# The second output projection of a two-layer encoder as seven block products

## The chip, the cores and the metric

The kernel runs on one core of one Trainium2 chip. The metric is the device time of one execution in microseconds, a median of runs. Engines are named as in the profile: PE (TensorE matmul) with PEld (its weight loads), DVE (VectorE), ACT (ScalarE), POOL (GpSimd), SP (SyncE, which here only issues DMAs).

## What is computed

A trunk of two layers over a sequence of 1024 rows and a width of 1024. Each layer normalizes its input, modulates it with a vector made from c, runs a token mixer, multiplies by a SiLU gate, projects with a 1024x1024 matrix and adds the gated result to its input. Layer 0 mixes by differential attention, layer 1 by latent attention with 8 heads of 128. A last normalization closes the trunk:

```python
for i in range(DEPTH):
    shift, scale, gate = _modulation(c, ada_w[i], ada_b[i])
    h = _rmsnorm(x, norm_g[i]) * (1.0 + scale) + shift
    ...
        y = _mla(h, positions, w_in1, q_a_norm_g, w_q_b, kv_a_norm_g, w_kv_b, w_out1)   # ends in  o @ w_out
    x = x + gate * y
return _rmsnorm(x, final_norm_g)
```

The change concerns `o @ w_out1`, `x + gate * y` and the last normalization of layer 1. Here o (1024 x 1024) lies as eight heads of 128 features; the first 512 rows are called half 0, the others half 1.

## The kernel before

All matmuls with fp32 data are done as three products of split numbers: a value is rounded to fp32r (hi) and the rest (lo) kept, and `mm3` (L184 to L187) issues hi*hi, hi*lo and lo*hi into one accumulator bank. So every operand has to be split once: ACT casts it to hi, POOL or DVE subtracts to get lo. One step of `mm3` on a 128x128 piece of o and a 128x512 piece of the matrix is three matmuls of 128x512.

Layer 1's attention goes head by head. A head has two halves, a half four score tiles of 128 rows. A tile's work is: scores on PE (L1704), maximum on DVE (L400), exponential on ACT (L402), transposes on PE into one bank `tr` (L383), hi of the transposed tile on ACT (L385, `pth`), lo on DVE (L386, `ptl`), product with v on PE (`pv`). Between these PE does steps of the projections of the next head (`acc`, the weights split by L230 on ACT into `wh` and by L231 on POOL into `wl`). After each half the output o is scaled on POOL (L885), split (ACT L890, POOL L891), and stored to DRAM as hi and lo (`oS`). A generator is advanced once per score tile; it computes the gate vector of layer 1 in pieces (DVE L424) and ends about halfway through the heads.

During the last head `extra1` loads half 0 of o from `oS` and splits the first pieces of w_out1, and `Pre` does the first five contraction steps of two accumulators in PE's order beside that head's attention. `late1` and `tail1` finish the last half of the last head without DRAM: 1/z is made into a diagonal (`dg`), spread by a matmul with ones (`rb`, L904) and multiplied in.

Then `out_proj` runs over row halves (gi), column halves (f) and heads (h): four accumulators `oacc` of 128x512, and for each of the 4 x 8 pieces of the matrix a load (`wor`, L1088), a cast (`woh`, L1104) and a subtraction (`wol`, L1105). So each piece of w_out1 is loaded and split twice, once for each row half. When four accumulators are complete, DVE multiplies each with the gate (`oy`, L1152) and adds it to the residual `xfull` (L1153); `done1` squares and sums it on ACT (L1829), multiplies by the final gain on POOL (L1836), makes the reciprocal root in seven tiny DVE instructions (L178, L180, L181), scales one column half on DVE (L1843) and the other on ACT (L1850), and stores both. In the last quarter (`LAST`) the row tiles are done two together, then one, then the last tile in two pieces of 256 columns.

Every engine works through one queue in order; the order is made when the program is built, by a list scheduler that keeps to what `behind` (L192) and `in_turn` (L196) prescribe: some POOL instructions stay in program order, and casts on ACT go behind the attention's last marked cast or exponential. DMAs are issued by SP, which waits in order too.

Of the kernel before, what the change touches and what calls it, by code (L numbers as in the profile page):

```python
# [11 lines left out]
F32 = mybir.dt.float32  # L12
# [35 lines left out]
OT1_AT = 5  # L48
NORM_AT = 4
PRE0 = (0, 0, 0, 0, 0, 0, 1, 1, 1, 2, 1)  # L50
PRE1 = (0,0,0,0,0,0,1,1,1,1,1)
OW0 = (3, 4)
OP0 = (6, 4)
OW1 = (2, 4)
OP1 = (12, 4)
LAST = [(((0, 1, 2, 3), 0, HF),), (((0, 1), 0, HF), ((2,), 0, HF), ((3,), 0, 256), ((3,), 256, HF))]
# [30 lines left out]
def trunk(ctx: ExitStack, tc: tile.TileContext, A, out):  # L87
# [49 lines left out]
    oS = [dr.tile([NH, 2, 2, P, HF], F32, name=f"oS{l}") for l in range(2)]  # L137
# [46 lines left out]
    def mm3(psum, ah, al, bh, bl, first, last):  # L184
        PE.matmul(psum, ah, bh, start=first, stop=False)  # L185
        PE.matmul(psum, ah, bl, start=False, stop=False)  # L186
        mm3.last = PE.matmul(psum, al, bh, start=False, stop=last).ins  # L187
# [691 lines left out]
    def finish(o, y, l, h, half, dst, ap_, dgs):  # L879

        if dst is None:
# [6 lines left out]
            def split():  # L888
                with behind("S"):
                    S.copy(b.bitcast(F32R), o)  # L890
                in_turn(G.tensor_sub(o.bitcast(F32R), o, b))  # L891
                SP.dma_start(oS[l][h, half, 0], b)
                SP.dma_start(oS[l][h, half, 1], o)
# [6 lines left out]
        rb = bank("m", "rb")  # L900
# [4 lines left out]
        V.tensor_mul(o, o, rb)  # L905
        hi, lo = dst
# [219 lines left out]
    def out_proj(OT, ow, W0, pre, wpool, xpool, nlate, nx, xsrc, tile_done, group_done):  # L1126
# [4 lines left out]
        for gi in range(2):  # L1131
# [5 lines left out]
            for f in range(2):  # L1137
# [9 lines left out]
                last = gi == 1 and f == 1  # L1147

                def resid(i, a=0, b=HF, acc=None):
                    y = wpool.tile([P, HF], F32, name="oy", tag="oy", bufs=2)  # L1150
                    cs = slice(f * HF + a, f * HF + b)
                    V.tensor_mul(y[:, a:b], (acc or accs[i])[:, a:b], ow.gb[:, cs])  # L1152
                    add = V.tensor_add(fulls[i][:, cs], fulls[i][:, cs], y[:, a:b])  # L1153
                    tile_done(gi * 4 + i, fulls[i], cs.start, cs.stop, add)

                if last:
                    for tiles, a, b in LAST[ow.l]:
                        part = None
                        if a:
                            part = bank("acc", "oaccb")  # L1160
                        for h in range(NH):
                            for i in tiles:
                                mm_o(part or accs[i], OT, W, h, gi, i, slice(a, b))
                            if h % 2 or len(tiles) == 4:
                                side.tick()
# [770 lines left out]
```

## Time and profile before

| | us |
|---|---|
| median of 3 runs | 1436.38 (1433.73 to 1439.55) |
| the profiled execution | 1437.65 |
| its span in the profile | 1435.9 |
| PE busy | 1398.5 (97%) |
| DVE, ACT, POOL busy | 921.5, 727.2, 612.9 |

Numbers in the profile come from one execution; its time is 1.27 above the median of the runs, and 1.75 lie outside the span. In a group of instructions the first number is the time they were busy, the second the mean of one in ns. In a row of the timeline the first number is the start in us from the span's start, the second the duration. Matmuls overlap (the next begins before the one before has ended), so the price of a matmul on PE is the distance of two starts, not the duration. A number in square brackets is how long the engine stood idle just before, and for whom.

### The profile page before, as it was taken

Reading aid. Unit: us, or ns where it says so; the run is one execution under the profiler, and the core shown is the slowest. Engines: PE = TensorE matmul, PEld = TensorE weight load, DVE = VectorE, ACT = ScalarE, POOL = GpSimd, SP = SyncE. Lnnn points to the kernel's source line nnn. Section 1 sums busy time; section 2 is a strip of 40 time slices with the busy share of each in tenths; the row PEclk is TensorE's granted clock in tenths of the full one; section 3 lists DMA queues with packets and bytes.
Section 4 is the critical chain, followed back from the end, with each engine's and each line's share of the span. In section 5 each row is a group of like instructions: output and inputs, shape, how many; then the busy total and the mean of one; then the engine's idle time right before and its main releaser. Section 6 shows DMA issues by size and latency. Waiting matters only on the chain. (4 is left out here: it accounts for less than half of the span.)

```text
span 1435.9 us, 20702 instructions
## 1 busy us (share of the span) xinstructions
PE 1398.5 (97%) x7426; PEld 1165.9 (81%) x7426; DVE 921.5 (64%) x1377; ACT 727.2 (51%) x1287; POOL 612.9 (43%) x485
## 2 busy tenths in 40 slices
PE   9999999999999999998999999999999999999997
PEld 6777788888888887887787877887888888888886
DVE  8655777777777767677345985545666555555356
ACT  5523465656565655566343442345454454545342
POOL 5425264646464655454552234531141331412572
PEclk9999999999999999999999999999999999999999
DMA  9776533334342324237653146398343433336563
GB/s 343 244 242 204 185 89 107 82 110 118 103 111 85 104 77 112 58 96 263 230 175 125 37 133 205 123 299 242 112 135 106 135 105 82 97 102 205 185 237 135
DMA packets 135385, 213.18 MB, mean 148 GB/s; under 512 B 19057, under 2 KB 56049, under 8 KB 135282
## 3 DMA queue, kind: packets, MB, share of 16 engines
q1 hardware_dynamic: 135282, 211.86, 47.8%
q8 instruction: 58, 0.95, 0.3%
q14 instruction: 45, 0.37, 0.1%
HBM read 137.40 MB, written 50.80 MB: 131 GB/s over the span
## 5 line engine op out<-in xcount | busy, mean ns | idle before, releaser
L385 ACT CAST pth<-tr 128x512 fp32r<-128x512 f32 x256 | 150.3, 587 | 284.9 <-PE tr L383 283.1
L400 DVE TENSOR_REDUCE nm<-s 128x1 f32<-128x1024 f32 x192 | 233.9, 1218 | 69.9 <-PE s L847 58.4
L386 DVE TENSOR_TENSOR ptl<-tr,pth 128x512 fp32r<-128x512 f32 x256 | 176.0, 688 | 140.3 <-ACT pth L385 140.0
L231 POOL TENSOR_TENSOR wl<-wraw,wh 128x512 fp32r<-128x512 f32 (+2 forms) x79 | 105.1, 1333 | 205.1 <-ACT wh L230 170.1
L402 ACT ACTIVATE e<-s,nm 128x1024 f32<-128x1024 f32 x128 | 143.6, 1122 | 30.8 <-DVE nm L400 28.4
L383 PE MATMUL tr<-ident,e 128*128 128x128 f32 x1024 | 155.0, 274 | 2.5 <-DVE ptl L386 2.4
L383 PEld LDWEIGHTS tr<-ident,e 128*128 128x128 f32 x1024 | 121.1, 140 | 43.6 <-DVE ptl L386 19.4
L185 PE MATMUL acc<-h0h,wh 128*128 128x512 f32 x360 | 150.1, 417 | 1.0 <-DVE v_hl L363 1.0
L185 PE MATMUL pv<-pth,vt 128*128 128x256 f32 x512 | 147.6, 288 | 0.9 <-DMA vt<-vS 0.9
L186 PE MATMUL pv<-ptl,vt 128*128 128x256 f32 x512 | 145.7, 284 | 0.0
L187 PE MATMUL pv<-pth,vt 128*128 128x256 f32 x512 | 144.7, 283 | 0.0
L187 PE MATMUL acc<-h0h,wl 128*128 128x512 f32 x360 | 143.2, 398 | 0.6 <-POOL wl L231 0.6
L186 PE MATMUL acc<-h0l,wh 128*128 128x512 f32 x360 | 142.0, 394 | 0.0
L1105 POOL TENSOR_TENSOR wol<-wor,woh 128x512 fp32r<-128x512 f32 x64 | 85.5, 1358 | 84.9 <-ACT woh L1104 84.3
L185 PEld LDWEIGHTS pv<-pth,vt 128*128 128x128 f32 x512 | 97.4, 190 | 4.3 <-issue 1.1
L186 PEld LDWEIGHTS pv<-ptl,vt 128*128 128x128 f32 x512 | 97.6, 191 | 2.7
L187 PEld LDWEIGHTS pv<-pth,vt 128*128 128x128 f32 x512 | 97.6, 191 | 0.0
L847 PE MATMUL s<-ks,qa 128*128 128x512 f32 x256 | 82.6, 404 | 6.1 <-DVE e L855 4.4
L327 POOL TENSOR_TENSOR rp_r<-rp_raw,cosT 128x512 f32<-128x512 f32 x38 | 50.0, 1316 | 85.6 <-ACT rp_raw L324 38.6
L332 POOL TENSOR_TENSOR rp_sw<-rp_sw,sinT 128x512 f32<-128x512 f32 x42 | 55.2, 1314 | 73.2 <-DMA rp_sw<-rp_raw 73.1
L855 DVE SCALAR_TENSOR_TENSOR e<-s,z,e 128x1024 f32<-128x1024 f32 x64 | 82.1, 1283 | 2.1
L187 PEld LDWEIGHTS acc<-h0h,wl 128*128 128x128 f32 x360 | 67.6, 188 | 16.3 <-POOL wl L231 1.0
(599 smaller groups left out, 3370.9 us busy)
## 6 DMA issues: line engine op xcount, KB each, us to landing
ada<-in_ada_ss SPq DMA_DIRECT2D x32, 512.0 KB, 5.6
wraw<-in_w_s SPq DMA_DIRECT2D x64, 256.0 KB, 2.9
vS<-v_hl SPq DMA_DIRECT2D x32, 512.0 KB, 5.9
vt<-vS SPq DMA_DIRECT2D x32, 512.0 KB, 3.9
wor<-in_w_out SPq DMA_DIRECT2D x64, 256.0 KB, 3.6
rp_sw<-rp_raw SPq DMA_DIRECT2D x168, 64.0 KB, 2.0
bc_s<-bc_d SPq DMA_DIRECT2D x34, 256.0 KB, 4.2
oS<-bc_s SPq DMA_DIRECT2D x30, 256.0 KB, 2.4
```

Of the source, the lines that this page charges most:

```text
L185: PE.matmul(psum, ah, bh, start=first, stop=False)
L186: PE.matmul(psum, ah, bl, start=False, stop=False)
L187: mm3.last = PE.matmul(psum, al, bh, start=False, stop=last).ins
L231: sub = (V if pair_of else G).tensor_sub(l_[:, :n], raw[:, :n], f32v(h_[:, :n]))
L383: PE.transpose(tr[:, j, :], p[:, kt * P : (kt + 1) * P], ident)
L385: mk["S"] = S.copy(pth[kh][:, :, dst], tr).ins
L386: mk["V"] = V.tensor_sub(ptl[kh][:, :, dst], tr, f32v(pth[kh][:, :, dst])).ins
L400: mk["V"] = V.reduce_max(nm, s_ps, axis=AX.X, negate=True).ins
L402: mk["S"] = S.activation(e, s_ps, AF.Exp, bias=nm, scale=1.0, accum_out=zs).ins
L847: PE.matmul(s_ps[:, kc * HF : (kc + 1) * HF], src[:, c, ql], KS[h][kc][:, c, :], start=fst, stop=not fst)
L855: combined.append(V.scalar_tensor_tensor(out=e0, in0=e1, scalar=z1[:, 0:1], in1=e0, op0=ALU.mult, op1=ALU.add).ins)
L1105: in_turn(G.tensor_sub(lo, raw, f32v(hi)))
```

## The change

The product o @ w_out1 is cut into 2x2 blocks: o into row halves and into heads 0 to 3 and 4 to 7 (A11, A12 of half 0, A21, A22 of half 1), w_out1 into rows of the same head groups and two column halves (B11 to B22). It is computed with seven block products of 512x512x512 instead of eight, on sums of blocks (Winograd's form of Strassen's method). A block product is 4 contraction steps by 4 row tiles.

- The gate is multiplied into w_out1 beforehand. In heads 3 to 6 of layer 1, in the steps of the generator that were empty, w_out1 is loaded once, POOL multiplies it with the gate (L1632) and forms four sums (L1637 to L1643), and the seven blocks are stored to DRAM unsplit (`tS`, 28 pieces). The pieces of o are no longer split at the end of a half but stored once, unsplit (`oF`); for two of the four head pairs POOL forms the four sums (`pair_steps`, L1659 to L1662) in the same steps and they are stored (`sS`).
- In the last head the operands of block 0 and most of block 1 are loaded straight into the buffers that will hold lo, cast on ACT (L1859) and subtracted on POOL in place (L1860); the sums for the third head pair are made there too, those of the fourth pair by four DVE instructions after the last half is complete. `Pre7` does four contraction steps of two accumulators there.
- After the attention the blocks follow each other: block 0 and 2 in accumulators Y, 1 in Z, 3 and 4 in Z, 5 and 6 in Y. Y and Z are added to the residual (L1977) and not cleared between 0 and 2, 3 and 4, 2, 5 and 6, so that a product enters every output it belongs to. While a block runs, the operands of the next one are split (parts of o by DVE, of the matrix by POOL) and those of the one after it fetched.
- There is no gate multiplication any more behind the accumulators. Row tiles 0 to 3 are complete after block 4 and get one common reciprocal root on POOL; tiles 4 to 7 come at the end as before, with four contraction steps to a tile.

Three places show how the order of the work is moved. POOL, heads 5 and 6, where the last key weights are split; `wl` 128x256 is their lo part, the rows above it rope work (`rp_`) and the scaling of a half's output. Before:

```order
L327 TENSOR_TENSOR rp_r<-rp_raw,cosT 128x512
L332 TENSOR_TENSOR rp_sw<-rp_sw,sinT 128x512
L885 TENSOR_TENSOR o_12321<-o_12321,bc_s 128x512
L231 TENSOR_TENSOR wl<-wraw,wh 128x256
L891 TENSOR_TENSOR o_12321<-o_12321,bc_s 128x512
```

After, at the same place (`ob` and `ot` are pieces of w_out1, `gb` is the gate):

```order
L327 TENSOR_TENSOR rp_r<-rp_raw,cosT 128x512
L1632 TENSOR_TENSOR ob<-ob,gb 128x512 x4
L332 TENSOR_TENSOR rp_sw<-rp_sw,sinT 128x512
L1637 TENSOR_TENSOR ob<-ob 128x512
L1638 TENSOR_TENSOR ot_12394<-ob 128x512
L885 TENSOR_TENSOR o_12384<-o_12384,bc_s 128x512
L1642 TENSOR_TENSOR ob<-ot_12394,ob 128x512
L1643 TENSOR_TENSOR ob<-ob,ot_12394 128x512
L231 TENSOR_TENSOR wl<-wraw,wh 128x256
```

Eight instructions now stand between the rope product and the split of the weights; the subtraction behind it is gone.

ACT in the last head, two score tiles. Before:

```order
L402 ACTIVATE e,zz_12927<-s_13033,nm 128x1024
L1104 CAST woh<-wor 128x512
L385 CAST pth<-tr 128x4x128
L402 ACTIVATE e,zz_12927<-s_13071,nm 128x1024
L385 CAST pth<-tr 128x4x128
L890 CAST bc_s<-o_13020 128x512
L1104 CAST woh<-wor 128x512
```

After:

```order
L402 ACTIVATE e,zz_13009<-s_13130,nm 128x1024
L1859 CAST oah<-oal 128x512
L1859 CAST woh<-wol 128x512
L385 CAST pth<-tr 128x4x128
L402 ACTIVATE e,zz_13009<-s_13173,nm 128x1024
L385 CAST pth<-tr 128x4x128
L1859 CAST oah<-oal 128x512
L1859 CAST woh<-wol 128x512
```

Between the exponential and the next cast of the transposes stand two operand casts where there was one.

DVE at the end of the program, from the residual addition of tile 6. Before (`tw` sums of squares, `rq_y` and `rq_t` the reciprocal root):

```order
L1152 TENSOR_TENSOR oy<-oacc,gb 128x512
L1153 TENSOR_TENSOR xfull<-xfull,oy 128x512
L1838 SCALAR_TENSOR_TENSOR tw_13463<-tss,tw_13463 128x1
L178 TENSOR_SCALAR rq_y<-tw_13463 128x1
L1152 TENSOR_TENSOR oy<-oacc,gb 128x256
L180 TENSOR_SCALAR rq_t<-tw_13463,rq_y 128x1
L1153 TENSOR_TENSOR xfull<-xfull,oy 128x256
```

After, from the same addition:

```order
L1977 TENSOR_TENSOR x_6_13561<-x_6_13561,oy 128x512
L180 TENSOR_SCALAR rq_t<-tw_13569,rq_y 128x1
L1977 TENSOR_TENSOR x_7_13562<-x_7_13562,oy 128x256
L181 SCALAR_TENSOR_TENSOR rq_y<-rq_t,rq_y 128x1
L2007 SCALAR_TENSOR_TENSOR x_5_13560<-x_5_13560,rq_y,fg 128x512
L1993 SCALAR_TENSOR_TENSOR tw_13570<-tss,tw_13570 128x1
L178 TENSOR_SCALAR rq_y<-tw_13570 128x1
L1977 TENSOR_TENSOR x_7_13562<-x_7_13562,oyb 128x256
```

The multiplication is gone; the roots of tiles 4 and 5 (`tw_13569`, `x_5`), which before stood ahead of tile 6's addition, now stand among the additions of the last tiles.

The diff, cut to its core:

```diff
-OT1_AT = 5
 NORM_AT = 4
 PRE0 = (0, 0, 0, 0, 0, 0, 1, 1, 1, 2, 1)
-PRE1 = (0,0,0,0,0,0,1,1,1,1,1)
+PRE1 = (0, 0, 0, 0, 0, 0, 0, 1, 1, 1, 1)
 OW0 = (3, 4)
 OP0 = (6, 4)
-OW1 = (2, 4)
-OP1 = (12, 4)
-LAST = [(((0, 1, 2, 3), 0, HF),), (((0, 1), 0, HF), ((2,), 0, HF), ((3,), 0, 256), ((3,), 256, HF))]
+LAST1 = (((0, 1), 0, HF), ((2,), 0, HF), ((3,), 0, 256), ((3,), 256, HF))
...
+    oF = dr.tile([NH, 2, P, HF], F32, name="oF")
+    tS = dr.tile([7, 4, P, HF], F32, name="tS")
+    sS = dr.tile([4, 2, P, HF], F32, name="sS")
...
            def split():
+                if l == 1:
+                    SP.dma_start(oF[h, half], o)
+                    return
                 with behind("S"):
                     S.copy(b.bitcast(F32R), o)
                 in_turn(G.tensor_sub(o.bitcast(F32R), o, b))
...
+        gb = [ut("gb", True, F32) for _ in range(2)]
+        for f in range(2):
+            SP.dma_start(gb[f], gateS[1][None, f * HF : f * HF + HF].to_broadcast([P, HF]))
+        for h in range(4):
+            (b11, b12), (b21, b22) = b_ = [[ap3.tile([P, HF], F32, name="ob", tag="ob", bufs=nob) for _ in range(2)] for _ in range(2)]
+            for m in range(2):
+                for f in range(2):
+                    SP.dma_start(b_[m][f], A["w_out1"][f, 4 * m + h])
+            yield
+            for f in range(2):
+                for m in range(2):
+                    in_turn(G.tensor_mul(b_[m][f], b_[m][f], gb[f]))
+            yield
+            for n, t in ((0, b11), (1, b21), (4, b22)):
+                SP.dma_start(tS[n, h], t)
+            t2 = ap3.tile([P, HF], F32, name="ot2", tag="ob", bufs=nob)
+            in_turn(G.tensor_sub(b12, b12, b11))
+            in_turn(G.tensor_sub(t2, b22, b12))
+            yield
+            for n, t in ((3, b12), (2, t2)):
+                SP.dma_start(tS[n, h], t)
+            in_turn(G.tensor_sub(b11, t2, b11))
+            in_turn(G.tensor_sub(b21, b21, t2))
+            yield
+            for n, t in ((5, b11), (6, b21)):
+                SP.dma_start(tS[n, h], t)
+            yield
+        yield from pair_steps(0)
+        yield
+        yield from pair_steps(1)
+    def pair_steps(h):
+        a = [ap3.tile([P, HF], F32, name="oa", tag="ob", bufs=nob) for _ in range(4)]
+        a11, a12, a21, a22 = a
+        for t, (hh, half) in zip(a, ((h, 0), (h + 4, 0), (h, 1), (h + 4, 1))):
+            SP.dma_start(t, oF[hh, half])
+        yield
+        in_turn(G.tensor_add(a22, a21, a22))
+        in_turn(G.tensor_sub(a21, a11, a21))
+        in_turn(G.tensor_sub(a11, a22, a11))
+        in_turn(G.tensor_sub(a12, a12, a11))
+        if h == 2:
+            for n, t in ((2, a11), (3, a22), (4, a12), (5, a21)):
+                sv.kept[n][2] = t
+        yield
+        for n, t in ((0, a22), (1, a11), (2, a21), (3, a12)):
+            SP.dma_start(sS[n, h], t)
+        yield
...
+        def home_a(self, n):
+            if n in (2, 3, 6):
+                return xt2k("oah"), xt2k("oal")
+            return [op.tile([P, HF], F32R, name="oa" + x_, tag="ab", bufs=16) for x_ in "hl"]
+        def home_w(self, n, h):
+            pl, tag, nb = (p6, "wp", 16) if n in (2, 3, 5) else (pw, "wo", 12) if n or h < 2 else (wst, "whl", 6)
+            return [pl.tile([P, HF], F32R, name="wo" + x_, tag=tag, bufs=nb) for x_ in "hl"]
+        def fetch_a(self, n, h):
+            if self.kept[n][h] is None:
+                self.raws[n, h, "A"] = self.load(self.home_a(n), oF[4 * (n > 0) + h, n // 6] if n in (0, 1, 6) else sS[(1, 0, 3, 2)[n - 2], h])
+        def fetch_w(self, n, h):
+            self.raws[n, h, "W"] = self.load(self.home_w(n, h), tS[n, h])
+        def load(self, home, src):
+            SP.dma_start(f32v(home[1]), src)
+            return *home, f32v(home[1])
+        def split_a(self, n, h, eng=V):
+            raw = self.kept[n][h]
+            hi, lo, raw = self.raws.pop((n, h, "A")) if raw is None else (*self.home_a(n), raw)
+            self.put(raw, hi, lo, eng)
+            self.A[n, h] = hi, lo
+        def split_w(self, n, h):
+            hi, lo, raw = self.raws.pop((n, h, "W"))
+            self.put(raw, hi, lo, G)
+            self.W[n, h] = hi, lo
+        def put(self, raw, hi, lo, eng):
+            with behind("S"):
+                S.copy(hi, raw)
+            sub = eng.tensor_sub(lo, raw, f32v(hi))
+            if eng is G:
+                in_turn(sub)
+        def fetch(self, n):
+            for h in range(4):
+                self.fetch_a(n, h)
+                self.fetch_w(n, h)
+        def splits(self, n):
+            for h in range(4):
+                self.split_a(n, h)
+                yield
+                self.split_w(n, h)
+                yield
+        def mm(self, n, acc, h, i, c=slice(0, HF), start=False):
+            (oh, ol), (wh, wl) = self.A[n, h], self.W[n, h]
+            r = slice(i * P, (i + 1) * P)
+            mm3(acc[:, c], oh[:, r], ol[:, r], wh[:, c], wl[:, c], start and h == 0, h == 3, True)
...
+        if i == 0:
+            for h in range(2):
+                fa(0, h)
+                fw(0, h)
+        if i == 1:
+            fa(0, 2)
+            fw(0, 2, 3)
+            SP.dma_start(a11_, oF[3, 0])
+            SP.dma_start(a21_, oF[3, 1])
+        if 1 <= i <= 4:
+            sv.split_a(0, i - 1, G)
+            sv.split_w(0, i - 1)
+        if i == 2:
+            fa(1, 0, 1, 2)
+        if i == 3:
+            fw(1, 0, 1)
+        if 4 <= i <= 5:
+            next(pair2, None)
+        if i == 5:
+            sv.split_a(1, 0, G)
+            sv.split_a(1, 1, G)
+            fw(1, 2, 3)
+        if i == 6:
+            sv.split_a(1, 2, G)
+            sv.split_w(1, 0)
+            fa(2, 0, 1)
+        if i == 7:
+            sv.split_w(1, 1)
...
+            for n, t in ((2, a11_), (3, dgs), (4, a12_), (5, a21_), (6, o)):
+                sv.kept[n][3] = t
+            V.tensor_add(dgs, a21_, o)
+            V.tensor_sub(a21_, a11_, a21_)
+            V.tensor_sub(a11_, dgs, a11_)
+            V.tensor_sub(a12_, a12_, a11_)
...
+    def add_to(tt, acc, f, a=0, b=HF, piece=False):
+        full = xs_[tt]
+        cs = slice(f * HF + a, f * HF + b)
+        add = V.tensor_add(full[:, cs], full[:, cs], acc[:, a:b])
+        if not piece:
+            return add.ins
+        early = tt // 4
         ss = sm.tile([P, 1], F32, name="tss")
         junk = p6.tile([P, HF], BF16, name="tjunk", tag="tjunk", bufs=1)
+        S.activation(junk[:, : b - a], full[:, cs], AF.Square, accum_out=ss)
+        final = f != early and b == HF
+        if final and tt == NT - 1:
             with tc.issue_after(add.ins):
                 held.pop()()
...
+    for h in range(2, 4):
+        sv.split_w(1, h)
+    sv.split_a(1, 3, G)
+    mk.clear()
+    for h in range(4):
+        sv.fetch_w(2, h)
+    sv.fetch_a(2, 2)
+    load_x1(0, 0)
+    Y = pre1.accs + [ps.tile([P, HF], F32, name="oy", tag="y", bufs=2) for _ in range(2)]
+    for h in range(4):
+        for i in range(2 if h < pre1.n else 0, 4):
+            sv.mm(0, Y[i], h, i, start=True)
+        if h == 2:
+            tail1()
+    SP.dma_start(fg, A["final_norm_g"].to_broadcast([P, D]))
+    for i in range(4):
+        add_to(i, Y[i], 0)
+    def step(gen, i):
+        for _ in range((3, 3, 2, 0)[i]):
+            next(gen)
+    Z = [bank("z", "oz") for _ in range(4)]
+    sp = sv.splits(2)
+    for h in range(4):
+        for i in range(4):
+            sv.mm(1, Z[i], h, i, start=True)
+        step(sp, h)
+        if h == 0:
+            G.tensor_scalar(fg, fg, -1.0 / 8192, None, op0=ALU.mult)
+        if h == 1:
+            sv.fetch(3)
+        if h == 2:
+            load_x1(0, 1)
+    for i in range(4):
+        add_to(i, Z[i], 0, piece=True)
+    sp = sv.splits(3)
+    for h in range(4):
+        for i in range(4):
+            sv.mm(2, Y[i], h, i)
+        step(sp, h)
+        if h == 1:
+            sv.fetch(4)
+        if h == 2:
+            load_x1(1, 1)
+    for i in range(4):
+        add_to(i, Y[i], 1)
+    Z = [bank("z", "oz") for _ in range(4)]
+    for n, first, rows, acc, f, piece in ((3, True, 4, Z, 1, False), (4, False, 0, Z, 1, True), (5, False, 4, Y, 1, True)):
+        sp = sv.splits(n + 1)
+        for i in range(4):
+            for h in range(4):
+                sv.mm(n, acc[i], h, i, start=first)
+            if n == 5 and i == 3:
+                a_ = LAST1[-1][1]
+                add_to(NT - 1, Y[3], 0, a_, HF)
+            add = add_to(rows + i, acc[i], f, piece=piece)
+            if n == 5:
+                with tc.issue_after(add):
+                    scale(i, y4[0][:, i : i + 1])
+            step(sp, i)
+            if i == 1 and n < 5:
+                sv.fetch(n + 2)
+            if i == 2 and n == 3:
+                load_x1(1, 0)
+    for tiles, a, b in LAST1:
+        acc = {i: bank("z", "oyb") if a else Y[i] for i in tiles}
+        for h in range(4):
+            for i in tiles:
+                sv.mm(6, acc[i], h, i, slice(a, b), start=a > 0)
+        for i in tiles:
+            add_to(4 + i, acc[i], 0, a, b, piece=True)
```

159 lines of the change are left out of this document (84 added, 75 removed).

## The prediction

> **What bounds the kernel now.** I read the page first, then the waits of PE in layer 1's attention and in the second output projection, then PE's timeline from the last product with v to the end.
>
> ```profile
> span 1435.9 us, 20702 instructions
> PE 1398.5 (97%) x7426; PEld 1165.9 (81%) x7426; DVE 921.5 (64%) x1377; ACT 727.2 (51%) x1287; POOL 612.9 (43%) x485
> PE   9999999999999999998999999999999999999997
> ```
>
> PE is the bound, in nearly every slice. So the first question of any change is how many matmuls it takes off PE, the second whether it makes PE wait. The waits of PE from 860 to 1344 us (attention), then from 1326 to 1436 (columns: total, times, longest):
>
> ```profile
> PE pv L185 <- DMA vt<-vS: 0.9, 1, 0.9
> ...
> PE tr L383 <- DVE ptl L386: 0.7, 1, 0.7
> ```
>
> ```profile
> PE oacc L186 <- POOL wol L1105: 0.7, 1, 0.7
> ```
>
> There is next to nothing to win from waits: the attention has two short waits of PE, on a load and on DVE, and the projection one on POOL. The timeline of PE around the projection:
>
> ```profile
> 1343.70 0.28 PE L187 MATMUL pv<-pth,vt 128*128 128x256 f32 x1
> 1343.82 0.39 PE L185 MATMUL oacc<-woh,o1a5h 128*128 128x512 f32 x1
> ...
> 1348.15 1.05 PE L904 MATMUL rb<-dg,ones 128*128 128x128 f32 x8
> 1348.96 0.48 PE L185 MATMUL oacc<-woh,o1a3h 128*128 128x512 f32 x1
> ...
> 1413.80 0.40 PE L185 MATMUL oacc<-woh,o1b7h 128*128 128x512 f32 x1
> 1414.90 0.50 PE L186 MATMUL oacc<-wol,o1b7h 128*128 128x512 f32 x1 [0.70 <-POOL wol L1105]
> ...
> 1427.30 0.28 PE L187 MATMUL oaccb<-woh,o1b7l 128*128 128x256 f32 x1
> ```
>
> The projection is 8 contraction steps x 8 row tiles x 2 column halves x 3 = 384 matmuls of 128x512 (the last tile's are issued as halves). Five steps of two tiles, 30 matmuls, run inside the last head, 354 after the last product with v. They go from 1343.82 to 1427.42 (the last start plus 0.12, a half's distance): 83.60 us. Off come rb, 0.81 (1348.15 to 1348.96), and the one gap, 1413.80 to 1414.90 less a step of 0.23, 0.87. The rest, 81.92, over 354 is 0.231 us a matmul.
>
> **The change, part by part.**
>
> *Seven blocks.* 7 x 4 steps x 4 tiles x 3 = 336 matmuls: 48 fewer, 48 x 0.231 = -11.1 us. 24 of them run in the last head (30 before), 312 after it; the total is what counts, since PE is full in both places.
>
> *The gap of 0.87.* It came from the second load and split of a late piece of the matrix. The pieces of the last block are now fetched when block 2 has freed their predecessors, two and a half blocks ahead of their use. -0.87, if the splits keep their lead.
>
> *Splits in the projection.* After the last head remain 40 casts on ACT; 23 subtractions, 8 gain products and one gain scaling on POOL; 17 subtractions, 4 sums and 29 additions on DVE. The groups from 1344 on (busy, mean ns):
>
> ```profile
> L1105 POOL TENSOR_TENSOR wol<-wor,woh 128x512 fp32r<-128x512 f32 x26 | 35.6, 1392 | 24.9 <-ACT woh L1104 24.3 <-DMA wor<-in_w_out 0.3
> L1836 POOL TENSOR_TENSOR xfull<-xfull,fg 128x512 f32<-128x512 f32 x8 | 11.9, 1520 | 0.0
> ```
>
> ```profile
> L1104 ACT CAST woh<-wor 128x512 fp32r<-128x512 f32 x24 | 14.7, 617 | 32.3 <-DMA wor<-in_w_out 22.8 <-PE oacc L186 5.1 <-PE oacc L187 2.3
> L1829 ACT ACTIVATE tjunk<-xfull 128x512 bf16<-128x512 f32 x15 | 9.5, 630 | 13.0 <-DVE xfull L1153 8.2 <-ACT tjunk L1829 1.8 <-DVE rq_y L181 1.0
> ```
>
> POOL: 23 x 1.39 + 8 x 1.52 = 44 us (and the scaling of the gain, which was there before) of the 73 that PE needs for its 312 matmuls and rb. ACT: 40 x 0.62 + 16 x 0.63 = 35, without the eight scalings. Both fit with a third to spare. For DVE the price depends on what runs beside it (groups from 1300 on, and one addition with POOL at rest):
>
> ```profile
> L1153 DVE TENSOR_TENSOR xfull<-xfull,oy 128x512 f32<-128x512 f32 x15 | 18.4, 1252 | 0.0
> ...
> L1152 DVE TENSOR_TENSOR oy<-oacc,gb 128x512 f32<-128x512 f32 x15 | 10.3, 688 | 24.3 <-PE oacc L187 24.3
> ```
>
> ```profile
> 1359.35 2.80 DVE L1153 TENSOR_TENSOR xfull<-xfull,oy 128x512 f32<-128x512 f32 x2
> 1424.38 0.69 DVE L1153 TENSOR_TENSOR xfull<-xfull,oy 128x512 f32<-128x512 f32 x1
> ```
>
> The addition of two SBUF tiles takes 0.69 alone and 1.40 in the pair at 1359.35, when POOL was splitting; the multiplication that reads an accumulator takes 0.69 always. The new additions read an accumulator: 29 x 0.69 = 20 us. The 17 subtractions and 4 sums have two SBUF inputs: 21 x 1.25 = 26, by the bounds 14.5 to 29. With eight scalings of 0.75 (row below) 52, and the tiny instructions of the roots, of some 80 us. [...]
>
> Whether the work fits in time as well: a block is 48 x 0.231 = 11.1 us. Block 1's operands are split in or just after the last head, blocks 2 and 3's within the 17 us of blocks 0 and 1, block n+1's during block n or earlier. DVE starts late (sums of the last half, 4 x 1.25, then five subtractions) and by my reckoning is some 4 us late with block 1's additions; their accumulators are needed again 11 us later, by block 3. Bounds for all block starts: 0 to 5 x 0.87 = 4.4 (each as bad as the one gap). I take 0.4, near the low end, because one gap in 32 splits is what the old order had with loads only three ahead.
>
> *Loads.* The matrix is loaded and split once instead of twice, so the projection has fewer of them:
>
> ```profile
> wor<-in_w_out SPq DMA_DIRECT2D x64, 256.0 KB, 3.6
> ```
>
> At 3.6 us to landing, a fetch a block and a half ahead (17 us) is no term. SP stands at block 5's fetches until block 2 is over; behind them wait the residual loads for blocks 5 and 6 and block 6's fetches, over 20 us ahead of use. 0.
>
> *Last head.* Two casts instead of one stand ahead of a cast of the transposes, at two or three places. ACT and PE there now:
>
> ```profile
> 1309.34 1.12 ACT L402 ACTIVATE e<-s,nm 128x1024 f32<-128x1024 f32 x1
> ...
> 1310.44 0.62 ACT L1104 CAST woh<-wor 128x512 fp32r<-128x512 f32 x1
> 1310.95 0.60 ACT L385 CAST pth<-tr 128x512 fp32r<-128x512 f32 x1
> ```
>
> ```profile
> 1310.29 0.60 PE L383 MATMUL tr<-ident,e 128*128 128x128 f32 x4
> ...
> 1312.52 0.60 PE L383 MATMUL tr<-ident,e 128*128 128x128 f32 x4
> ```
>
> A cast more moves `pth` from 1310.95 to 1311.46; it ends at 1312.06, `ptl` (0.69, as L1152) at 1312.75, and the next transposes stand at 1312.52. One more score matmul (0.23) now comes ahead of them, so they are due at 1312.75: the slack is just gone. Bounds 0 to 3 x 0.51 = 1.5; I take 0.3.
>
> *Heads 3 to 6.* POOL gets 40 instructions of 128x512 and loses the subtractions of the outputs' splits, 15 over all heads. Nothing waits for the new ones but SP; behind them wait the weight splits `wl`, for which PE waits. The tightest place, before:
>
> ```profile
> 1194.34 1.53 POOL L885 TENSOR_TENSOR o<-o,bc_s 128x512 f32<-128x512 f32 x1 [5.45 <-DVE o L1722]
> ...
> 1236.51 1.28 POOL L327 TENSOR_TENSOR rp_r<-rp_raw,cosT 128x512 f32<-128x512 f32 x1
> ...
> 1242.29 1.55 POOL L885 TENSOR_TENSOR o<-o,bc_s 128x512 f32<-128x512 f32 x1
> 1249.55 0.74 POOL L231 TENSOR_TENSOR wl<-wraw,wh 128x256 fp32r<-128x256 f32 x1 [5.71 <-ACT wh L230]
> ```
>
> ```profile
> 1254.73 0.39 PE L187 MATMUL acc<-ckh,wl 128*128 128x512 f32 x1
> ```
>
> From 1237.79 on POOL now does nine of 1.28 (4 + 2 + 2 new ones and a rope product) and L885, 1.55: the weights' turn comes at 1250.9, they are done at 1251.6, and PE wants them at 1254.73. 3.1 us of slack are left of 4.4. Elsewhere two to six new ones stand in front. Bounds 0 to 4 groups x 0.7 (a burst of four, 5.1, all of it behind the cast, against that lead of 4.4) = 2.8; I take 0.3. No gain is possible there: PE has no wait on POOL, ACT or SP to lose. SP gets some 45 DMAs more; it stands waiting now too, most of all for the row sums:
>
> ```profile
> SPq L408 <- DVE zz L1723: 75.5, 13, 9.3
> ```
>
> and the loads that PE needs stand behind such waits of up to 9.3 us without effect, so 0. That POOL can be fuller beside this attention shows in layer 0's (50 us of layer 0, then of layer 1; PE, PEld, DVE, ACT, POOL busy):
>
> ```profile
> 370.00:420.00 50.00, 49.93 (x283) 42.30 (x282) 39.56 (x58) 30.62 (x54) 32.42 (x28) 1.00 0.38 98
> ```
>
> ```profile
> 1200.00:1250.00 50.00, 50.00 (x310) 43.18 (x309) 27.35 (x37) 26.69 (x50) 15.76 (x13) 1.00 0.33 92
> ```
>
> A head lasts 48 us (the same output's scaling, L885, one head apart: 1194.34 and 1242.29), so 40 x 1.28 = 51 us in three and a half heads are 15 in 50: layer 1 comes to 31, under layer 0's 32.4, where PE lost 0.07.
>
> *After the last matmul.* The multiplication with the gate goes from the last tile's chain:
>
> ```profile
> 1419.52 0.15 DVE L1838 SCALAR_TENSOR_TENSOR tw<-tss,tw 128x1 f32<-128x1 f32 x1
> ...
> 1422.99 0.75 DVE L1843 SCALAR_TENSOR_TENSOR xfull<-xfull,rq_y,fg 128x512 f32<-128x512 f32 x1
> ...
> 1428.21 0.42 DVE L1152 TENSOR_TENSOR oy<-oaccb,gb 128x256 f32<-128x256 f32 x1
> 1428.66 0.42 DVE L1153 TENSOR_TENSOR xfull<-xfull,oy 128x256 f32<-128x256 f32 x1
> ...
> 1431.62 0.75 DVE L1843 SCALAR_TENSOR_TENSOR xfull<-xfull,rq_y,fg 128x512 f32<-128x512 f32 x1
> ```
>
> -0.45 (1428.21 to 1428.66). But a tile is now complete after four contraction steps instead of eight, so the last four tiles come half as far apart: the first two are ready 5.6 us (24 x 0.231) before the end, not 11.1. DVE needs for them 3 x 0.69 + 2 x 0.42 of additions and twice 4.2 us of roots and scaling (two tiles, 1419.52 to 1423.74): 11.3 from 6.2 before the last matmul ends, so to 5.1 after it without a gap, where it is 4.95 now (1432.37 less 1427.42). And the other tile's scaling, which before ran while ACT squared the last piece, now stands inside the last tile's chain. I take +0.7 in all; bounds -0.45 and +2.0 (the same work with a quarter of gaps).
>
> **Sum.** -11.1 - 0.87 + 0.4 + 0.3 + 0.3 + 0.7 = -10.3. The span comes to 1425.6, that execution to 1427.4 (1437.65 before). It lay 1.27 above the median of the runs, 1436.38: the forecast for the median is 1426.1, 0.7% less.
>
> **Rivals.** (1) *Slower: weight splits behind POOL's bursts.* If the four groups of eight (8 x 1.28 = 10.2 us) stand as a whole in front of a `wl`, because in_w_out lands late and POOL, in order, waits for it, PE waits 10.2 - 4.4 = 5.8 us at each: 1426.1 + 4 x 5.8 = 1449. It decides from about 3 us of delay beyond the order's count: each us more is one at up to four places, and with 6 us at each the gain is gone. For it: POOL waits in order, and the lead here falls to 3.1. Against: the loads are issued one score tile ahead of the products, with 3.6 us to landing, and most `wl` have fewer in front. 1 in 10.
> (2) *Splits become the bound between blocks*, so that the matmuls saved turn into waits at five block starts of 1 to 2 us: 1431 to 1436. For it: blocks 3 to 5 finish tile by tile and need all four steps' operands in their first 2.8 us, where the old order needed one new piece in 2.8 us. Against: POOL is busy for 44 of 73 us. [...] 15 in 100.
> (3) *Nothing in the way*: no price at all, 1436.38 - 11.1 - 0.87 - 0.45 = 1424.0. It lies in the forecast's own range.
> That the matmuls do not become fewer is excluded by the program, which has 348 instructions with 24 halves for them, 408 with 48 before.
>
> **Numbers.** Forecast with (3), 1422.5 to 1429: 75 in 100. (2): 15, (1): 10. The median of three runs can by itself lie some 1.5 off, hence 1422.5 below; upwards the range takes in the greater part of (2), to 1432. Half a percent, 7.2 us, is about what a measurement of this kernel tells from no change. Faster by more than that: 75 in 100, within: 15, slower: 10.
>
> **What will show it.** Right: after the last `pv`, 312 matmuls within 73 to 74 us, no wait of PE over 0.5 at a block's first four; the last matmul near 1416; 8.5 to 9.5 us behind it; attention ending at 1342 to 1343 (a pre-step of 1.4 fewer). Wrong: PE waiting for `wl` in heads 4 to 6, for `wol`, `oal` or `oah` at block starts, or for `ptl` in the last head; DVE's last scaling more than 6.5 us behind the last matmul.

## The result, and the profile after

The changed kernel takes 1429.33 us (median of 7 runs, 1427.78 to 1433.65); the kernel before, measured again beside it, 1436.98 (7 runs). The ratio is 0.9952, its 95% interval 0.9936 to 0.9968: 7.65 us or half a percent faster. The forecast was 1426.1, in a range of 1422.5 to 1432: the direction is right, and 2.65 us of the expected 10.3 are missing. The profiled execution took 1431.13 us. The head of its page, with PE's busy share and the granted clock in 40 slices:

```profile
span 1429.4 us, 20667 instructions
PE 1391.0 (97%) x7366; PEld 1160.0 (81%) x7366; DVE 933.0 (65%) x1368; ACT 729.8 (51%) x1295; POOL 658.7 (46%) x520
...
PE   8999999999999999998999999999999999999997
...
PEclk8999999999999999999999999999999999999999
```

PE is the bound as before, with 7.5 us less to do and a span 6.5 us shorter. Where the difference lies is read from PE's timeline at five places: the first scores of the second head, those of the last head (start, duration), the last product with v, the last matmul. Before (the last two rows of before stand in the prediction: 1343.70 and 1427.30):

```profile
1016.05 0.39 PE L1704 MATMUL s<-kn_h,qn_h 128*128 128x512 f32 x1
...
1293.74 0.39 PE L1704 MATMUL s<-kn_h,qn_h 128*128 128x512 f32 x1
```

After:

```profile
1016.52 0.39 PE L1740 MATMUL s<-kn_h,qn_h 128*128 128x512 f32 x1
...
1294.24 0.39 PE L1740 MATMUL s<-kn_h,qn_h 128*128 128x512 f32 x1
...
1347.74 0.28 PE L187 MATMUL pv<-pth,vt 128*128 128x256 f32 x1
...
1420.69 0.28 PE L187 MATMUL oyb<-woh,oal 128*128 128x256 f32 x1
```

| stretch | before | after | difference | forecast for it |
|---|---|---|---|---|
| up to the second head | 1016.05 | 1016.52 | +0.47 | 0 |
| second to seventh head | 277.69 | 277.72 | +0.03 | +0.3 |
| last head, to the last product with v | 49.96 | 53.50 | +3.54 | -1.4 + 0.3 |
| from there to the last matmul | 83.60 | 72.95 | -10.65 | -9.7 - 0.87 + 0.4 |
| from there to the end of the span | 8.60 | 8.71 | +0.11 | +0.7 |

The first row is not read as an effect of the change: the first scores of layer 1 lie anywhere between 969.4 and 975.9 us in the eleven profiles of this study, and single executions of one kernel differ by some 5 us. So what follows is read by stretches, in which the profiles agree to 0.2 us. One row is far off: the last head. The waits of PE from 1326 to 1436 us (total, times, longest), where before there was only the 0.7 for `wol`:

```profile
PE tr L383 <- DVE ptl L386: 2.4, 1, 2.4
```

The rows around that wait, engine by engine:

```profile
1324.11 1.30 POOL L1659 TENSOR_TENSOR oa<-oa 128x512 f32<-128x512 f32 x1
...
1326.85 1.29 POOL L1661 TENSOR_TENSOR oa<-oa 128x512 f32<-128x512 f32 x1
```

```profile
1328.17 0.62 ACT L1859 CAST oah<-oa 128x512 fp32r<-128x512 f32 x1 [2.53 <-POOL oa L1661]
1328.70 0.58 ACT L385 CAST pth<-tr 128x512 fp32r<-128x512 f32 x1
```

```profile
1328.82 1.21 DVE L1860 TENSOR_TENSOR oal<-oa,oah 128x512 fp32r<-128x512 f32 x1 [2.75 <-ACT oah L1859]
1329.95 0.68 DVE L386 TENSOR_TENSOR ptl<-tr,pth 128x512 fp32r<-128x512 f32 x1
```

```profile
1327.88 0.40 PE L1740 MATMUL s<-kn_l,qn_h 128*128 128x512 f32 x1
1330.69 0.65 PE L383 MATMUL tr<-ident,e 128*128 128x128 f32 x4 [2.41 <-DVE ptl L386]
...
1331.99 1.05 PE L1740 MATMUL s<-kps,qpa 128*128 128x512 f32 x2
1332.85 1.05 PE L1740 MATMUL s<-kps,qpb 128*128 128x512 f32 x2
```

ACT stands 2.53 us in front of the cast of `oa`, a sum of a pair of heads that POOL makes as the third of four. Behind that cast waits `pth`, which has long had its transposes; on DVE the subtraction belonging to the cast comes ahead of `ptl`; and PE waits for `ptl`. After the pause two matmuls take 0.86 us (1331.99 to 1332.85) where two take 0.46 elsewhere. The windows view (PE, PEld, DVE, ACT, POOL busy, then the granted clock) says why:

```profile
1330.00:1335.00 5.00, 4.31 (x18) 3.65 (x19) 3.51 (x5) 2.93 (x6) 5.00 (x4) 0.67 0.05 19
```

A clock of 0.67 over 5 us is 3.3 us at half speed.

The cast has no business in the last head. It splits an operand of block 2, which PE first uses at 1371, 40 us later. In the program it stands in block 1, but there `behind` prescribes nothing any more (`mk.clear()` comes ahead of the blocks), its source was ready early, and the list scheduler put it here.

The projection itself went as written. From 1360 to 1390 DVE and POOL were full, and still PE never waited there:

```profile
1360.00:1390.00 30.00, 30.00 (x131) 24.29 (x130) 29.67 (x32) 16.23 (x34) 27.96 (x18) 1.00 0.70 249
```

### The profile page after: what moved, and what is told of

Read it like the earlier page. It is cut to its first block, busy times and chain, and to the rows that moved or that the text cites. A ratio compares the mean times of both kernels' runs of the same rounds, so it can differ in the third digit from the quotient of the medians.

```text
span 1429.4 us, 20667 instructions
## 1 busy us (share of the span) xinstructions
PE 1391.0 (97%) x7366; PEld 1160.0 (81%) x7366; DVE 933.0 (65%) x1368; ACT 729.8 (51%) x1295; POOL 658.7 (46%) x520
## 5 line engine op out<-in xcount | busy, mean ns | idle before, releaser
L231 POOL TENSOR_TENSOR wl<-wraw,wh 128x512 fp32r<-128x512 f32 (+2 forms) x79 | 104.9, 1330 | 212.8 <-ACT wh L230 183.1
L847 PE MATMUL s<-ks,qb 128*128 128x512 f32 x256 | 80.2, 394 | 0.0
```

The source lines that it names most:

```text
L231: sub = (V if pair_of else G).tensor_sub(l_[:, :n], raw[:, :n], f32v(h_[:, :n]))
L847: PE.matmul(s_ps[:, kc * HF : (kc + 1) * HF], src[:, c, ql], KS[h][kc][:, c, :], start=fst, stop=not fst)
```

## The experiments

The last head's length (first scores to last product with v) in all of them, with PE's longest wait in it, how long the clock was at half there, the time, and the median of the kernel before that was measured beside it:

| kernel | last head, us | longest wait there | at half clock | time, us | before beside it |
|---|---|---|---|---|---|
| before (6 matmuls of 0.231 more) | 49.96 | none | 0 | 1436.98 | |
| after | 53.50 | 2.41 | 3.41 | 1429.33 | 1436.98 |
| subtraction moved later | 51.32 | 1.79 | 0 | 1428.69, one run | 1434.92 |
| two POOL instructions more | 57.74 | 5.31 | 6.83 | 1436.34, one run | 1434.92 |
| the split pinned | 53.51 | 2.34 | 3.41 | 1428.87 | 1434.92 |
| the split pinned, `dg` on ACT | 49.65 | 0.5 | 0 | 1425.45 | 1438.13 |
| fewer matmuls in the blocks | 53.62 | 2.41 | 3.41 | 1426.03, one run | 1434.92 |
| more POOL work in heads 3 to 6 | 52.54 | 2.41 | 0 | 1433.04, one run | 1438.13 |
| pin and `dg`, splits a tile later | 49.58 | 0.1 | 0 | 1429.89, one run | 1438.13 |
| pin and `dg`, tiles 4 and 5 apart | 49.49 | 0.1 | 0 | 1425.40, one run | 1438.13 |
| pin and `dg`, roots on POOL | 49.47 | 0.1 | 0 | 1428.16, one run | 1437.01, one run |

All three kernels that leave the cast, its subtraction and POOL's work ahead of it as they were (after, fewer matmuls, more POOL work in heads 3 to 6) show the same wait of 2.41; the stretch at half clock follows it in two of them only. The last section comes back to that.

### The subtraction alone moved off the last head

```diff
             with behind("S"):
                 S.copy(hi, raw)
-            sub = eng.tensor_sub(lo, raw, f32v(hi))
+            with tc.issue_after(self.hold) if raw is self.kept[2][2] else nullcontext(): sub = eng.tensor_sub(lo, raw, f32v(hi))
...
-    mk.clear()
+    sv.hold = mk["V"]; mk.clear()
```

> Only the subtraction of that split is moved off DVE's last head; the cast stays where it was on ACT. Theory A: of the wait of 2.41, DVE's subtraction ahead of ptl made 0.7 and ACT's wait the rest, so a wait of 1.7 stays. [...] Theory B: the wait stays at 2.4.

PE at the same transposes, and the stretch behind them:

```profile
1329.63 0.66 PE L383 MATMUL tr<-ident,e 128*128 128x128 f32 x4 [1.79 <-DVE ptl L386]
```

```profile
1330.00:1335.00 5.00, 5.00 (x35) 4.25 (x34) 3.61 (x6) 4.32 (x8) 5.00 (x5) 1.00 0.15 57
```

The wait is 1.79: theory A's division, 0.6 of 2.41 for DVE's subtraction and the rest for ACT's wait, is right. The clock stays at 1.00, and the last head is 2.18 us shorter than after, of which the wait explains 0.62. The other 1.56 is what the slow stretch cost. The kernel with more POOL work in heads 3 to 6 gives the same: its last head has the wait of 2.41 too and 0.60 more of another wait, but no slow stretch, and is 0.96 shorter than after.

### More work ahead of the pair sum

```diff
-        in_turn(G.tensor_sub(a11, a22, a11))
-        in_turn(G.tensor_sub(a12, a12, a11))
+        for _ in range(2 * (h == 2)): in_turn(G.tensor_scalar(a12, a12, 1.0, None, op0=ALU.mult))
+        in_turn(G.tensor_sub(a11, a22, a11)); in_turn(G.tensor_sub(a12, a12, a11))
```

> Two more POOL instructions of 128x512 (a multiplication by 1, some 1.4 us each) ahead of the pair sum for which ACT waits. Theory A: the wait of PE grows from 2.4 by 2.8 to 5.2 us. If the half speed lasts for one window whatever the pause, the slow stretch stays at 3.4 us; if every idle window is followed by a slow one, it becomes two windows, and up to 1.5 us more are lost: 1432 to 1434. If POOL is not the cause: nothing changes, 1429 to 1430.

```profile
1334.84 1.11 PE L383 MATMUL tr<-ident,e 128*128 128x128 f32 x4 [5.31 <-DVE ptl L386]
```

```profile
1332.32 0.62 ACT L1859 CAST oah<-oa 128x512 fp32r<-128x512 f32 x1 [5.43 <-POOL oa L1662]
```

```profile
1330.00:1335.00 5.00, 0.16 (x1) 0.16 (x2) 2.03 (x3) 1.10 (x2) 4.92 (x4) 0.86 0.00 2
1335.00:1340.00 5.00, 5.00 (x17) 4.22 (x18) 2.63 (x3) 2.89 (x6) 4.83 (x5) 0.50 0.24 65
```

ACT's wait and PE's wait grew by 2.9 us with POOL's work (two instructions of 1.5), so POOL's sum is what the chain hangs on. The slow stretch became two of 3.4 us, the first of them partly within the pause. The last head is 4.24 us longer than after, 2.9 by the wait and 1.3 by the clock. The one time, 1436.34, lies above the expected range; by the stretch it would be 1433.6, inside it.

### The split pinned behind the attention

```diff
-    mk.clear()
+    sv.hold = mk["S"]; mk.clear()
...
         def put(self, raw, hi, lo, eng):
-            with behind("S"):
+            with tc.issue_after(self.hold) if raw is self.kept[2][2] else behind("S"):
                 S.copy(hi, raw)
```

> One edit: the split of the third pair sum for block 2 may no longer stand in the last head, its cast on ACT comes behind the last cast of the transposes. PE's order is unchanged. Theory A (ACT stood in order behind this cast, which waited 2.53 us for POOL's pair sum; PE then waited 2.41 us for ptl and ran one clock window at half speed): the wait and the half-speed window are gone, 2.4 + 1.5 = 3.9 us less, a time of about 1425.4, the ratio to before near 0.992, no wait of PE over 0.5 in the last head. Theory B (POOL itself is too full in the last head with its sums and splits): the wait turns up at the next operand, less than 1 us is won, 1428.5 to 1429.5.

The ratio to before is 0.9947 (0.9926 to 0.9968, 6 runs against 9): by the time nothing is won. ACT's wait for the pair sum is gone from the profile, and yet PE waits 2.34 us, three transposes later:

```profile
1339.31 1.11 PE L383 MATMUL tr<-ident,e 128*128 128x128 f32 x4 [2.34 <-DVE ptl L386]
```

```profile
1334.65 4.01 DVE L906 TENSOR_SCALAR dg<-ident,zz 128x128 f32<-128x128 f32 x4
1338.58 0.68 DVE L386 TENSOR_TENSOR ptl<-tr,pth 128x512 fp32r<-128x512 f32 x1
```

```profile
1334.81 1.30 POOL L1860 TENSOR_TENSOR oal<-oal,oah 128x512 fp32r<-128x512 f32 x1
1336.08 2.50 POOL L1860 TENSOR_TENSOR wol<-wol,woh 128x512 fp32r<-128x512 f32 x2
```

The four `dg` of the last half's 1/z ran while POOL was splitting and took 4.01 us: the first, which started before POOL's subtraction, 0.29, the other three 1.30 to 1.33 each. In the kernel after, where the first wait had held everything up and they met POOL at rest (its next instruction starts at 1338.64 after 2.20 us of idling), they took 0.88:

```profile
1336.73 0.88 DVE L906 TENSOR_SCALAR dg<-ident,zz 128x128 f32<-128x128 f32 x4
```

```profile
1338.64 1.29 POOL L1860 TENSOR_TENSOR wol<-wol,woh 128x512 fp32r<-128x512 f32 x1 [2.20 <-ACT woh L1859]
```

So theory A was right on the first wait and wrong that it was the last; theory B, room on POOL as such, fits the time but not these rows. The six runs lie between 1425.42 and 1432.39, so perhaps the two did not meet in each; there is a profile of one of them only.

### The split pinned, and `dg` made on ACT

```diff
-            V.tensor_scalar(dgs[:, js], ident, y[:, j : j + 1], None, op0=ALU.mult)
+            S.mul(dgs[:, js], ident, y[:, j : j + 1]) if l else V.tensor_scalar(dgs[:, js], ident, y[:, j : j + 1], None, op0=ALU.mult)
```

> The pinned split as before, and the four products ident x 1/z (dg, 128x128) are made on ACT instead of DVE. Theory C: with the first wait gone, the second came from DVE, whose four dg took 1.31 us each beside POOL's subtractions (one such subtraction is 1.3) where they take 0.28 with POOL at rest. Without them on DVE no wait of PE over 0.6 is left in the last head and no window at half speed: from the first scores of layer 1 to the last product with v 371.5 us (375.3 in the kernel after, 375.4 with the pin alone), a median of about 1425, a ratio to before of 0.992 to 0.994. Rival: the last head is short of room on ACT and POOL as such; then a third wait takes their place, 375 us again and 1428 to 1429.

The median is 1425.45 (1423.75 to 1427.65, 4 runs), the ratio to before, measured beside it, 0.9907 (0.9891 to 0.9924). From the first scores of layer 1 to the last product with v it takes 371.49 us, as expected. PE's only wait in the last head:

```profile
PE tr L383 <- DVE ptl L386: 0.5, 1, 0.5
```

```profile
1335.15 0.99 ACT L906 ACTIVATE dg<-ident,zz 128x128 f32<-128x128 f32 x3
```

No stretch of the last head is below a clock of 1.00. The last head takes 49.65 us, 3.85 less than in the kernel after; the three further kernels with both edits have 49.47 to 49.58. The interval lies below that of the changed kernel (0.9936 to 0.9968), each against the kernel before, so this version is faster than both kernels.

### Fewer matmuls, the same splits

```diff
+            if n in (1, 2, 3): PE.matmul(acc[:, c], oh[:, r], wh[:, c], start=start and h == 0, stop=False, skip_group_check=True); return PE.matmul(acc[:, c], oh[:, r], wl[:, c], start=False, stop=h == 3, skip_group_check=True)
             mm3(acc[:, c], oh[:, r], ol[:, r], wh[:, c], wl[:, c], start and h == 0, h == 3, True)
```

> Leaves out the lo*hi matmul in blocks 1, 2 and 3, 48 matmuls or 11.1 us, with all splits and additions kept. In the profile after, the splits are ready 8.6 to 17 us ahead of their use there, least for the matrix parts of block 4. If the splits have this lead and their order does not depend on PE: PE waits about 2.5 us at block 4 and 8.6 us are won. If they start earlier with PE, since its matmuls free their buffers: no wait and 11.1 us. If the splits bound the blocks (the rival of the prediction): waits at several block starts, and less than 5 us are won.

```profile
1381.72 0.50 PE L186 MATMUL oz<-wol,oah 128*128 128x512 f32 x1 [0.51 <-POOL wol L1860]
...
1383.41 0.50 PE L186 MATMUL oz<-wol,oah 128*128 128x512 f32 x1 [0.72 <-POOL wol L1860]
...
1384.64 0.50 PE L186 MATMUL oz<-wol,oah 128*128 128x512 f32 x1 [0.27 <-POOL wol L1860]
```

From the last product with v to the last matmul it takes 64.18 us instead of 72.95: 8.77 of the 11.1 left out are won, with PE idle at block 4 for POOL, 1.5 us in three places (the 2.33 that are missing are more than this idle time, as the gap of 0.70 in the kernel before cost 0.87). That is the first of the three expectations (8.6). The blocks of the changed kernel are bound by PE; the splits would bind if PE came to block 4 more than some 8.7 us earlier.

### More POOL work in heads 3 to 6

```diff
-            yield
+            yield [in_turn(G.tensor_scalar(b22, b22, 1.0, None, op0=ALU.mult)) for _ in range(2)]
             for n, t in ((0, b11), (1, b21), (4, b22)):
```

> The kernel after with two more POOL instructions (multiplications by 1, 128x512, 1.4 us each) behind each of the four groups of gate multiplications in heads 3 to 6. At the tightest place the weights' split ends at 1252.3 there and PE uses it at 1255.2, a lead of 2.9 us. If POOL's bursts are hidden up to that lead: 2.8 fit just in, a wait of at most 0.2, the time as the kernel after's. If the burst has a price of its own from the first instruction on: 0.5 us and more per group.

```profile
1163.46 0.50 PE L187 MATMUL acc<-ckh,wl 128*128 128x512 f32 x1 [0.71 <-POOL wl L231]
...
1215.35 0.50 PE L187 MATMUL acc<-ckh,wl 128*128 128x512 f32 x1 [1.67 <-POOL wl L231]
...
1257.97 0.50 PE L187 MATMUL acc<-ckh,wl 128*128 128x512 f32 x1 [0.16 <-POOL wl L231]
```

The expectation held at the place it was worked out for (0.16 at 1257.97) and failed at two others; the second to seventh head take 280.98 us instead of 277.72, and the one time is 1433.04. What was overlooked is that SP passes the delay on. Its rows in the kernel after, and with the added work:

```profile
1179.23 4.08 SPq L1635 DMA_DIRECT2D tS<-ob  x3
...
1193.05 0.38 SPq L209 DMA_DIRECT2D wraw<-in_w_qn  x1
```

```profile
1182.75 7.21 SPq L1635 DMA_DIRECT2D tS<-ob  x3
...
1199.81 0.38 SPq L209 DMA_DIRECT2D wraw<-in_w_qn  x1
```

SP stands at the stores of the gated pieces until POOL has made them (three stores in 7.21 us instead of 4.08), and the weights' load behind them starts at 1199.81 instead of 1193.05, 6.8 us later for about 3 us of work in each of two groups. The row sums' load for L885 is late with it, and POOL's next group begins at 1206 instead of 1199, in front of a `wl` that before had a clear POOL.

### Splits one score tile later, and two other ends

```diff
-        if 1 <= i <= 4:
-            sv.split_a(0, i - 1, G)
-            sv.split_w(0, i - 1)
+        if 2 <= i <= 5:
+            sv.split_a(0, i - 2, G)
+            sv.split_w(0, i - 2)
...
-        if i == 5:
+        if i == 6:
             sv.split_a(1, 0, G)
...
-        if i == 6:
+        if i == 7:
             sv.split_a(1, 2, G)
```

> Pin and dg on ACT, and the splits of block 0 and of block 1's first parts stand one score tile later. In the profile after, two of them on ACT wait for their loads (0.20 and 1.12 us) and PE comes 0.53 us late at the transposes behind them, of 0.86 in all from such casts. If late loads are the reason: first scores to last product 0.5 us shorter than with pin and dg alone. If it is only that two casts stand in a row: no change within 0.2.

The last head takes 49.58 us, against 49.65 with pin and `dg` alone, and the stretch that the expectation names 371.69 against 371.49: late loads cost nothing worth naming. (The one time, 1429.89, is 4.4 above the median with pin and `dg` alone. Its profile is 2.2 longer than the other's, and 2.0 of that lies ahead of the first scores of layer 1.) About 1 us more than 49.96 less 1.39 (the six matmuls moved out) remains, and stays put down to the casts without being shown.

```diff
-LAST1 = (((0, 1), 0, HF), ((2,), 0, HF), ((3,), 0, 256), ((3,), 256, HF))
+LAST1 = (((0,), 0, HF), ((1,), 0, HF), ((2,), 0, HF), ((3,), 0, 256), ((3,), 256, HF))
```

> Pin and dg on ACT, and in the last block tiles 4 and 5 are done one after the other, not together; PE's work is the same. If DVE's roots and scalings of tiles 4 and 5 are what stands inside the last tiles' chain: they start 2.8 us earlier, and DVE's last instruction ends 4.0 us after the start of the last matmul instead of 4.9. If the last tile's own chain sets the end: 4.7 to 4.9 as before.

```diff
-            scale(tt, rsqrt8k(w)[:, 0:1])
+            y = rsqrt8k(w) if tt > 5 else rsqrt(w, 1); tt > 5 or G.tensor_scalar(y, y, -8192.0, None, op0=ALU.mult); scale(tt, y[:, 0:1])
```

> Pin and dg on ACT, and the reciprocal roots of tiles 4 and 5 are made on POOL, which rests there, by its power instruction (1.04 us for four columns in the profile after) instead of seven tiny instructions each on DVE; 14 instructions of 0.15 to 0.28 us leave DVE's end chain. If DVE's work behind the last tiles sets the end: DVE's last instruction ends 4.3 us or less after the start of the last matmul instead of 4.9. If the last tile's own chain (addition, square on ACT, root, scaling) sets it, or DVE now waits for POOL as long as it worked before: 4.7 to 5.1.

DVE's last instruction in the two, the last matmul starting at 1414.52 and 1416.54:

```profile
1419.07 0.75 DVE L2007 SCALAR_TENSOR_TENSOR x<-x,rq_y,fg 128x512 f32<-128x512 f32 x1
```

```profile
1421.89 0.75 DVE L2007 SCALAR_TENSOR_TENSOR x<-x,rq_y,fg 128x512 f32<-128x512 f32 x1
```

It ends 5.30 and 6.10 us after the start of the last matmul, where it is 4.86 in the kernel after, 4.87 with pin and `dg` alone, and was 5.07 before. Both guesses failed. In both kernels DVE's list has tile 6's scaling ahead of nearly all of the last tile's root, where the kernel after works on the two roots in turn; so the order of the tiny instructions at the end seems to matter more than how many there are; that wasn't tried by itself.

## Why the prediction was right, and where it was wrong

- *The matmuls* (-11.1) and *the gap* (-0.87): right. Behind the last product with v stand 312 matmuls and `rb` in 72.95 us; 42 x 0.231 = 9.7 and 0.87 of the 10.65 are gone there, and the six others in the last head.
- *Block starts* (+0.4, bounds 0 to 4.4): nothing. PE waits nowhere in the blocks, and rival (2) did not come, though its "for" was better than I knew: POOL's "third to spare" holds for the 73 us together (47.35 busy), not for 1360 to 1390, where POOL and DVE are full: POOL's subtractions took 1.67 us in the mean there (1.29 alone), nine of DVE's 1.44 (0.69 alone). What saved it is the lead of 8.6 to 8.8 us that the kernel with fewer matmuls shows.
- *Heads 3 to 6* (+0.3, bounds 0 to 2.8) and rival (1): +0.03 in the profile. The size is right, the reason only half. I took one tight place, with a lead of 3.1 (2.9 measured), for the tightest, and I let SP's waits cost 0 for whatever length. With some 3 us more in each group PE waits at other places, and the price is 3.3 us.
- *After the last matmul* (+0.7): +0.1, well below the forecast and within its bounds.
- *Last head* (+0.3, bounds 0 to 1.5): this is the step that failed. The stretch lost 3.54 us instead of winning 1.1. Two casts in a row instead of one were priced, by their durations, and about 1 us of what was lost may be theirs. The third cast in that stretch was not seen to be another thing: it is of block 2, not of block 0 or 1, and its source is a sum that POOL makes behind four other instructions. "Nothing waits for the new ones but SP" was said of POOL's work in heads 3 to 6; for the same sums in the last head the reader of ACT's row had to ask it again. With it went the bound: a cast that waits has no upper bound of 0.51. It cost 2.41 of waiting and some 1.5 of half speed, together 3.9 of the 4.6 us by which this stretch came out above its forecast; the other 0.8 stays put down to the casts. Of the forecast's own signs of being wrong this one came: PE waiting for `ptl` in the last head.
- The clock was in no term of the sum; in the kernel after, 3.41 us at a clock of 0.50 followed the pause of 2.41.
- *The range.* The time lies inside it, but above 1429, up to which the forecast reached without rival (2). The room above was there for waits between the blocks, which did not come; a wait in the last head filled it. In that respect the range held by luck.

## What to carry to other kernels

When a change moves instructions onto an engine that works in order, list for each of them what it waits for, not how long it takes: a cast of 0.6 us in the wrong place held up PE by 2.4 us. A scheduler that may move work freely behind a fence will also move it ahead of it; pin what feeds a later stage. And when one wait is taken away, look in the new profile for the next one before judging by the time: here the second was nearly as long as the first (2.34 and 2.41) and had been covered by it.

## What the runs showed of the hardware that I had not expected

*Half speed after a pause.* In the kernel after, PE's pause of 2.41 us (1328.28 to 1330.69) was followed by a granted clock of 0.50 from 1331.72 to 1335.13, that is for 3.41 us; of the 3.41 us just ahead of that stretch PE was idle for 2.38. In the kernel with more POOL work in heads 3 to 6 a pause of the same length ended 3.30 us later, and the clock stayed full:

```profile
1333.99 0.66 PE L383 MATMUL tr<-ident,e 128*128 128x128 f32 x4 [2.41 <-DVE ptl L386]
```

```profile
1330.00:1335.00 5.00, 2.59 (x14) 1.86 (x13) 2.87 (x3) 1.42 (x3) 4.84 (x5) 1.00 0.01 2
1335.00:1340.00 5.00, 5.00 (x36) 4.35 (x35) 3.61 (x8) 4.63 (x10) 4.75 (x4) 1.00 0.34 107
```

Behind the 1.79 of the moved subtraction the clock was 1.00 from 1330 to 1345. Behind a pause of 1.79 early in the profile of the pinned split it was 0.50:

```profile
891.10 0.50 PE L187 MATMUL zacc<-t2h,wl 128*128 128x512 f32 x1 [1.79 <-POOL wl L231]
```

```profile
892.00:895.00 3.00, 3.00 (x9) 2.32 (x8) 0.84 (x1) 0.15 (x1) 3.00 (x3) 0.50 0.26 87
```

So the length of a pause alone did not decide here, and what else did is not shown. The slow stretch cost about 1.5 us (1.56 above), so the same wait of 2.41 cost 3.9 in the kernel after and 2.4 in the one with more POOL work.

*DVE beside POOL.* `dg`, a multiplication of 128x128 with one SBUF input and a scalar for each row, took 0.28 us with POOL at rest and, in three of four, 1.30 to 1.33 beside POOL's subtractions, which took 1.26 to 1.30 each. Where DVE and POOL both ran subtractions of two SBUF inputs, from 1360 to 1390, both took longer (mean in ns of one; DVE 690 alone, POOL 1290):

```profile
L1860 DVE TENSOR_TENSOR oal<-oal,oah 128x512 fp32r<-128x512 f32 x9 | 12.8, 1437 | 0.3 <-ACT oah L1859 0.3
...
L1860 DVE TENSOR_TENSOR oal<-o1k,oah 128x512 fp32r<-128x512 f32 x2 | 3.6, 1781 | 0.0
```

```profile
L1860 POOL TENSOR_TENSOR wol<-wol,woh 128x512 fp32r<-128x512 f32 x13 | 21.3, 1671 | 0.1
```

The prediction's upper bound for such a subtraction, 1.40, taken from one pair of additions, was too low. POOL's subtractions started 1.66 to 1.70 us apart there (1360.41, 1362.07, 1363.77), one of DVE's with each. That is less than 0.69 + 1.29 = 1.98; how much the two overlapped, and how much is only that a record runs some hundredths into the next, is open. DVE's additions that read an accumulator, which the forecast put at 0.69 whatever runs beside them, took 0.67 in the same stretch.
